# Value and output-gate projections as seven half-block products in an early stage of a hybrid encoder block

## The chip, the cores and the metric

The kernel runs on one core of a Trainium2 chip. The metric is the device time of one launch in microseconds (us); the runs shown are given by their median. TensorE (PE in the profile) multiplies matrices into PSUM, an on-chip memory of eight banks of 128 x 512 fp32. VectorE (DVE) and ScalarE (ACT) do the elementwise work, GpSimd (POOL) and SyncE (SP) issue most of the transfers between DRAM and the on-chip SBUF.

## The reference: one hybrid encoder block

One layer over 512 positions of width 1024 in fp32. Three branches share one normalised input `h`; all their inputs come out of one wide projection. What this change touches are `sb_v`, `ml_v`, `ml_o` (1024 columns each), `ml_i`, `ml_f` (4 columns each) and the second third of `gate_pre`.

```python
h = _rmsnorm(x, g_mix[l])
z = h @ w_in[l]
(sb_q, sb_k, sb_v, ml_q, ml_k, ml_v, ml_o, ml_i, ml_f, x_q, gate_pre) = jnp.split(z, IN_SPLITS, axis=-1)
y_sb = stick_breaking(8 heads of 128: sb_q, sb_k, sb_v)
qk = jax.nn.silu(_causal_conv(jnp.concatenate([ml_q, ml_k], axis=-1), conv_w[l], conv_b[l]))
...
hm = _mlstm(4 heads of 256: mq, mk, ml_v, i_pre, f_pre)
hm = _rmsnorm(hm, ml_norm_g)
y_ml = hm * jax.nn.sigmoid(ml_o)
y_x = cross_attention(4 heads of 256: x_q, 256 memory tokens)
gates = jax.nn.sigmoid(gate_pre + b_gate[l]).reshape(bsz, seq, N_BRANCH, D_MODEL)
mixed = gates[:, :, 0] * (y_sb @ w_sb_proj) + gates[:, :, 1] * (y_ml @ w_ml_proj) + gates[:, :, 2] * (y_x @ w_x_proj)
x = x + mixed @ w_out[l]
u = _rmsnorm(x, g_mlp[l]) @ w_ff1[l]
x = x + jnp.square(jax.nn.relu(u)) @ w_ff2[l]
```

## The kernel before: one long queue of matmuls

Every fp32 operand is kept as a pair of a high and a low half (`whi`, `wlo` for weights, two planes of `h` for the input). ACT makes the high half by a copy, DVE the low half by a subtraction (`load_w`, L81 and L82; `split`, L93 and L94, with a scale L96 and L97). A product is then three matmuls, high by high, high by low and low by high (`mm3`, L86 to L88). A projection in the form `projT` gives 128 features x 512 positions in 24 matmuls of 512 columns. In the form `projN` it gives 512 positions x 256 features in 96 matmuls of 256 columns, with `h` as the stationary operand; the twelve calls of `projN` are the values of two stick-breaking heads each (`sb_v`, four), the mLSTM values (`ml_v`, four) and the mLSTM output gate (`ml_o`, four).

The stages follow each other on PE: keys and values of the memory tokens (to 56 us); cross-attention with its query projections `xq` and the third branch's gates (to 154); their output projection with the first branch's gates (to 220); stick-breaking, eight heads (to 417); the first branch's output projection (to 484); mLSTM, four heads (to 718); the second branch's output projection with four of its gates (to 785); then the last projection and the MLP, which already use seven half-block products in place of eight, by the function `product` (L735 to L737).

An mLSTM head consists of four query and key feature tiles f0 to f3 (`ml_qk`: projection into a bank `pj`, copied by ACT into `xs` at L608; a four-tap convolution into `u`, one step on ACT (L609) and three on DVE (L612); a sigmoid; the split `mqk`), the scores `st` with their decay `w`, `sc`, the numerators `nm`, a norm, and the product with the sigmoid of the output gate. The code of a head starts the next head's feature tiles before its own numerators, and the output-gate and value projections of the next head behind them. In head 3, gates of the second branch stand in both places. The input and forget gates are computed as eight further columns of the first `sb_v` projection, gathered in `gcol` and transposed ahead of mLSTM.

The program is written in the order of the stages; a scheduler with buffers of fixed number (`tag`, `bufs`) sets the order on each engine, and each engine then works strictly in that order. PSUM has two banks `pj`, four `q4` and two `tr`.

Of the kernel before, what the change touches and what calls it, by code (L numbers as in the profile page):

```python
# [15 lines left out]
P = 128  # L16
# [10 lines left out]
NI = HD + 8  # L27
WI = 4 * NI

# [7 lines left out]
def tile_block(ctx: ExitStack, tc: tile.TileContext, xT, x_, memT, mem_, small,  # L37
               w_sbqk, w_sbv0, w_sbv, w_mlqk, w_mlv, w_mlo, w_xq, w_gate, w_kv,
# [33 lines left out]
    def load_w(src, parts=1, raw=None):  # L72
        n = src.shape[-1]
        if raw is None:
            raw = wp.tile([P, WI], F32, tag="raw", bufs=3, name="raw")
        hi = wp.tile([P, WI], F32R, tag="whi", bufs=4, name="whi")
        lo = wp.tile([P, WI], F32R, tag="wlo", bufs=4, name="wlo")
        for i in range(parts):
            c = slice(i * n // parts, (i + 1) * n // parts)
            nc.sync.dma_start(out=raw[:, c], in_=src[:, c])  # L80
            act.activation(out=hi[:, c], in_=raw[:, c], func=AF.Copy)  # L81
            dve.tensor_tensor(out=lo[:, c], in0=raw[:, c], in1=f32(hi[:, c]), op=ALU.subtract)  # L82
        return hi, lo
# [29 lines left out]
    def projN(wsrc, out_of, n=HD):  # L113

        ws = [load_w(wsrc[c]) for c in range(2)]
        for i in range(NT):
            out = out_of(i)
            for k in range(NK):
                hi, lo = ws[k // 4]
                c = slice((k % 4) * n, (k % 4 + 1) * n)  # L120
                mm3(out, h[k][:, 0, i * P:(i + 1) * P], h[k][:, 1, i * P:(i + 1) * P],
                    hi[:, c], lo[:, c], k == 0, k == NK - 1)

# [15 lines left out]
    def sigmoid(out, src, b=0.0, nb=0.0):  # L139
# [5 lines left out]
        act.activation(out=out, in_=out, func=AF.Exp, bias=b)  # L145

# [31 lines left out]
    gcol = cp.tile([P, NT, 64], F32, tag="gcol", name="gcol")  # L178
    pool.memset(gcol, 0.0)
# [9 lines left out]
    def mem_tiles(c):  # L189
        mT = hp.tile([P, 2, M], F32, tag="gate", bufs=4, name="mT")  # L190
# [66 lines left out]
    def mem_k(g):  # L257
# [9 lines left out]
        for m in range(NM):  # L267
            r = rk[:, 2 * m:2 * m + 2]
            dve.tensor_scalar(out=r, in0=r, scalar1=rm[:, m:m + 1], scalar2=None, op0=ALU.mult)
            t = hp.tile([P, T], F32, tag="gate", bufs=4, name="kn")  # L270
# [30 lines left out]

    mixed = [None] * NK

    def gate(b, f):
        o = pj()
        projT(h, load_w(w_gate[b * NK + f]), o)
        g = hp.tile([P, T], F32, tag="gate", bufs=4, name="gate")
# [127 lines left out]
    def sb_v(g):  # L435
        vs[g] = [tp.tile([P, 2, HD], F32R, tag="v", bufs=6, name="v") for _ in range(NT - 1)]
        vs[g].append(tp.tile([P, HD], F32, tag="v3", bufs=2, name="v3"))
        if g == 0:

            po = [q4() for _ in range(NT)]  # L440
            projN(w_sbv0, lambda i: po[i][:, :NI], NI)
            for i in range(NT):
                sb_vi(g, i, po[i][:, :HD])
                dve.tensor_copy(out=gcol[:, i].rearrange("p (a b) -> p a b", a=2)[:, :, :4],
                                in_=po[i][:, HD:NI].rearrange("p (a b) -> p a b", a=2))
            return
        po = [pj(), pj()]
        projN(w_sbv[g - 1], lambda i: po[i // 2][:, (i % 2) * HD:(i % 2 + 1) * HD])
        for i in range(NT):
            sb_vi(g, i, po[i // 2][:, (i % 2) * HD:(i % 2 + 1) * HD])  # L450
# [67 lines left out]
    sb_v(0)  # L518
    sb_qk(0)
    sb_weights(0)  # L520
    gs, aT = [], None
# [19 lines left out]

    o = tr()
    for i in range(NT):
        pe.transpose(o[:64, i * P:(i + 1) * P], gcol[:, i], ident)
    ip, fp, fa, mf, fc = (tmp(n)[:4, :] for n in ("ip", "fp", "fa", "mf", "fc"))
    act.activation(out=ip, in_=o[0:4, :], func=AF.Identity, bias=sm[0:4, C_BIF:C_BIF + 1])
    act.activation(out=fp, in_=o[32:36, :], func=AF.Identity, bias=sm[32:36, C_BIF:C_BIF + 1])
# [33 lines left out]
    def ml_v(head):  # L581
        vs[head] = []
        po = [pj(), pj()]
        projN(w_mlv[head], lambda i: po[i // 2][:, (i % 2) * HD:(i % 2 + 1) * HD])
        for i in range(NT):
            t = tp.tile([P, 2, HD + 2], F32R, tag="v", bufs=8, name="v")
            split(t[:, 0, :HD], t[:, 1, :HD], po[i // 2][:, (i % 2) * HD:(i % 2 + 1) * HD])
# [3 lines left out]
    def ml_o(head):  # L591
        po = [tr(), tr()]
        projN(w_mlo[head], lambda i: po[i // 2][:, (i % 2) * HD:(i % 2 + 1) * HD])
        sos[head] = []
        for b in range(2):
            t = tp.tile([P, T], F32, tag="so", bufs=4, name="so")
            sigmoid(t, po[b])
            sos[head].append(t)

    def ml_qk(head):  # L600
        qk = qks.setdefault(head, [])
        for f in range(4):
# [3 lines left out]
            u, xs = tmp("u"), tmp("xs")  # L606
            cw = C_CW + 4 * ft
            act.activation(out=xs, in_=o, func=AF.Copy)  # L608
            act.activation(out=u, in_=xs, func=AF.Identity, scale=sm[:, cw + 3:cw + 4],  # L609
                           bias=sm[:, C_CB + ft:C_CB + ft + 1])  # L610
            for d in (1, 2, 3):
                dve.scalar_tensor_tensor(out=u[:, d:], in0=xs[:, :T - d], scalar=sm[:, cw + 3 - d:cw + 4 - d],  # L612
# [24 lines left out]
    for head in range(4):  # L637
# [32 lines left out]
        else:  # L670
            gs += [gate(1, 0), gate(1, 1)]
# [19 lines left out]
        yts = [tmp("yt") if head == 3 else hp.tile([P, T], F32, tag="gate", bufs=4, name="yt") for _ in range(2)]  # L691
        for i in range(NT):
            c = slice((i % 2) * HD, (i % 2 + 1) * HD)
            dve.scalar_tensor_tensor(out=yts[i // 2][:, c], in0=nms[i][:, :HD], scalar=dn[:, i:i + 1],
                                     in1=so[i // 2][:, c], op0=ALU.mult, op1=ALU.mult)
        if head < 3:
            ml_o(head + 1)
            ml_v(head + 1)
        else:
            gs += [gate(1, 2), gate(1, 3)]  # L700
# [10 lines left out]
    def w_pair(raw):  # L711
        hi = wp.tile([P, WI], F32R, tag="whi", bufs=4, name="whi")
        lo = wp.tile([P, WI], F32R, tag="wlo", bufs=4, name="wlo")
        act.activation(out=hi[:, :W], in_=raw, func=AF.Copy)  # L714
        dve.tensor_tensor(out=lo[:, :W], in0=raw, in1=f32(hi[:, :W]), op=ALU.subtract)  # L715
        return hi, lo

    def s_new():

        return [hp.tile([P, 4, 2 * P], F32R, tag="h", bufs=NK, name=n) for n in ("shi", "slo")]  # L720

    def s_pair(src):
        sp = s_new()
        split(*sp, src)
        return sp

    def product(banks, sp, ws, start, stop, after=lambda v: None, end=False):

        def one(j, k, c):
            st, sp_ = start and k == 0, stop and k == 3  # L730
            lh, ll = sp[0][:, k, j * P:(j + 1) * P], sp[1][:, k, j * P:(j + 1) * P]
            w = ws[k // 2]
            cw = slice((k % 2) * T + c.start, (k % 2) * T + c.stop)
            mm = dict(skip_group_check=True)
            pe.matmul(banks[j][:, c], lh, w[0][:, cw], start=st, stop=False, **mm)  # L735
            pe.matmul(banks[j][:, c], lh, w[1][:, cw], start=False, stop=False, **mm)  # L736
            pe.matmul(banks[j][:, c], ll, w[0][:, cw], start=False, stop=sp_, **mm)  # L737

        if end:

            for j, c in ((0, slice(0, T)), (1, slice(0, T // 2)), (1, slice(T // 2, T))):
                for k in range(4):
                    one(j, k, c)
            return
        for v in range(2):
            for j in range(2):
                for k in (2 * v, 2 * v + 1):
# [342 lines left out]
```

## Time and profile before

| | us |
|---|---|
| median of three runs | 1165.07 (1164.43 to 1166.15) |
| the profiled execution, its own time | 1165.21 |
| its span in the trace | 1162.8 |
| PE busy | 1153.2 (99%) |
| DVE busy | 709.7 (61%) |
| ACT busy | 641.1 (55%) |
| twelve head-wise projections, stretches on PE | 137.2 |
| mLSTM stage, 484 to 718 | 234.0 |

The granted TensorE clock is 0.999 of full speed in this execution. The trace gives each instruction's start and duration. On PE neighbouring matmuls overlap, so a group's summed duration is more than the time it takes; the length of a stretch of the timeline is the better measure. For DVE and ACT, too, the distance between two starts in a row is shorter than the duration shown (by about 0.1 us). Times are counted from the start of the span.

### The profile page before, as it was taken

How to read it: one execution, taken by the hardware profiler on the slowest of the kernel's cores; microseconds unless marked ns; L12 is line 12 of the kernel's file. 1: busy time of each engine (PE TensorE's matmuls, PEld its weight loads, DVE VectorE, ACT ScalarE, POOL GpSimd, SP SyncE). 2: the span in 40 equal slices, each digit the busy share in tenths (PEclk: the TensorE clock that was granted, in tenths of full speed). 3: DMA queues.
4: the chain of work that ended last, by engine and by line, in shares of the span. 5: the costliest groups of instructions: out<-in, count | busy, mean ns of one | idle time of the engine just before them, and what ended most of it. 6: DMA issues, size and time to landing. Idle time of an engine off the chain costs nothing.

```text
span 1162.8 us, 15156 instructions
## 1 busy us (share of the span) xinstructions
PE 1153.2 (99%) x5844; PEld 970.9 (83%) x5844; DVE 709.7 (61%) x1112; ACT 641.1 (55%) x1085; POOL 58.5 (5%) x100
## 2 busy tenths in 40 slices
PE   9999999999999999999999999999999999999998
PEld 6788888888988888898989898888888888888887
DVE  5966633357567753475677765479638448458457
ACT  7955544246556754276767666445645354454443
POOL 0000000000000000010000000001001001011010
PEclk9999999999999999999999999999999999999999
DMA  9631223232222222323222225648547548448244
GB/s 361 225 115 45 73 81 102 73 109 74 73 74 73 73 91 93 93 78 109 82 91 79 86 73 178 206 109 207 165 96 177 170 106 200 145 102 208 89 72 109
DMA packets 40687, 138.45 MB, mean 119 GB/s; under 512 B 4516, under 2 KB 4900, under 8 KB 40616
## 3 DMA queue, kind: packets, MB, share of 16 engines
q1 hardware_dynamic: 34712, 116.45, 30.0%
q0 software_dynamic: 5760, 20.97, 10.2%
q8 instruction: 46, 0.75, 0.3%
q14 instruction: 25, 0.20, 0.1%
q10 hardware_dynamic: 144, 0.07, 0.0%
HBM read 135.37 MB, written 2.11 MB: 118 GB/s over the span
## 4 chain that ended last, share of the span: by engine, by line
PE 94%; DMA 2%; DVE 2%; ACT 1%; issue 1%; SPq 0%; DVEq 0%; ACTq 0%
PE pj L88 16%; PE pj L87 16%; PE pj L86 16%; PE q L86 7%; PE q L87 6%; PE q L88 6%; PE q L737 3%; PE q L736 3%; PE q L735 3%; PE tr L86 2%; PE tr L88 2%; PE tr L87 2%; PE pj L737 2%; PE pj L736 2%; PE pj L735 2%; DMA xrow<-in_x_dram 1%
## 5 line engine op out<-in xcount | busy, mean ns | idle before, releaser
L82 DVE TENSOR_TENSOR wlo<-raw,whi 128x1024 fp32r<-128x1024 f32 x148 | 180.6, 1223 | 209.3 <-ACT whi L81 197.7
L81 ACT ACTIVATE whi<-raw 128x1024 fp32r<-128x1024 f32 x148 | 156.3, 1060 | 240.4 <-PE pj L87 159.5
L86 PE MATMUL pj<-h,whi 128*128 128x512 f32 x512 | 202.4, 395 | 0.0
L87 PE MATMUL pj<-h,whi 128*128 128x512 f32 x512 | 201.3, 393 | 0.0
L88 PE MATMUL pj<-h,wlo 128*128 128x512 f32 x512 | 201.2, 393 | 0.0
L714 ACT ACTIVATE whi<-rq 128x1024 fp32r<-128x1024 f32 x70 | 74.3, 1061 | 110.5 <-PE q L87 43.6
L715 DVE TENSOR_TENSOR wlo<-rq,whi 128x1024 fp32r<-128x1024 f32 x70 | 85.5, 1221 | 76.1 <-ACT whi L714 75.9
L88 PEld LDWEIGHTS pj<-h,wlo 128*128 128x128 f32 x512 | 96.3, 188 | 21.0 <-issue 0.5
L86 PEld LDWEIGHTS pj<-h,whi 128*128 128x128 f32 x512 | 96.5, 189 | 20.0
L87 PEld LDWEIGHTS pj<-h,whi 128*128 128x128 f32 x512 | 96.3, 188 | 19.9
L88 PE MATMUL q<-x1g,wlo 128*128 128x512 f32 x240 | 94.2, 393 | 0.0
L86 PE MATMUL q<-x1g,whi 128*128 128x512 f32 x240 | 94.2, 392 | 0.0
L87 PE MATMUL q<-x1g,whi 128*128 128x512 f32 x240 | 94.1, 392 | 0.0
L86 PE MATMUL pj<-y,whi 128*128 128x512 f32 x192 | 75.8, 395 | 0.0
L88 PE MATMUL pj<-y,wlo 128*128 128x512 f32 x192 | 75.6, 394 | 0.0
L87 PE MATMUL pj<-y,whi 128*128 128x512 f32 x192 | 75.5, 393 | 0.0
L737 PE MATMUL q<-whi,slo 128*128 128x512 f32 (+1 forms) x164 | 63.5, 387 | 0.0
L735 PE MATMUL q<-whi,shi 128*128 128x512 f32 (+1 forms) x164 | 63.5, 387 | 0.0
L736 PE MATMUL q<-wlo,shi 128*128 128x512 f32 (+1 forms) x164 | 63.4, 387 | 0.0
L86 PE MATMUL pj<-whi,h 128*128 128x256 f32 x224 | 63.3, 283 | 0.0
L88 PE MATMUL pj<-whi,h 128*128 128x256 f32 x224 | 63.1, 282 | 0.0
L87 PE MATMUL pj<-wlo,h 128*128 128x256 f32 x224 | 63.0, 281 | 0.0
(344 smaller groups left out, 2372.2 us busy)
## 6 DMA issues: line engine op xcount, KB each, us to landing
raw<-in_w_ff_dram SPq DMA_DIRECT2D x32, 512.0 KB, 3.7
rq<-in_w_ff_dram SPq DMA_DIRECT2D x32, 512.0 KB, 5.1
rq<-in_w_ff_dram POOLq DMA_DIRECT2D x32, 512.0 KB, 5.4
raw<-in_w_gate_dram SPq DMA_DIRECT2D x24, 512.0 KB, 3.5
raw<-in_w_proj_dram SPq DMA_DIRECT2D x24, 512.0 KB, 3.6
raw<-in_w_sbqk_dram SPq DMA_DIRECT2D x16, 512.0 KB, 3.5
raw<-in_w_mlqk_dram SPq DMA_DIRECT2D x16, 512.0 KB, 3.5
rawk<-in_w_kv_dram SPq DMA_DIRECT2D x10, 512.0 KB, 9.0
```

Of the source, the lines that this page charges most:

```text
L81: act.activation(out=hi[:, c], in_=raw[:, c], func=AF.Copy)
L82: dve.tensor_tensor(out=lo[:, c], in0=raw[:, c], in1=f32(hi[:, c]), op=ALU.subtract)
L86: pe.matmul(out, lh, rh, start=start, stop=False)
L87: pe.matmul(out, lh, rl, start=False, stop=False)
L88: pe.matmul(out, ll, rh, start=False, stop=stop)
L714: act.activation(out=hi[:, :W], in_=raw, func=AF.Copy)
L715: dve.tensor_tensor(out=lo[:, :W], in0=raw, in1=f32(hi[:, :W]), op=ALU.subtract)
L735: pe.matmul(banks[j][:, c], lh, w[0][:, cw], start=st, stop=False, **mm)
L736: pe.matmul(banks[j][:, c], lh, w[1][:, cw], start=False, stop=False, **mm)
L737: pe.matmul(banks[j][:, c], ll, w[0][:, cw], start=False, stop=sp_, **mm)
```

## The change: an early stage, three matrices at once

Behind the memory keys and ahead of the query projections stands a new stage that computes three matrices of 512 x 1024, `sb_v`, `ml_v` and `ml_o`, each as a product of `h` with a 1024 x 1024 weight. Both are cut into two halves each way, and the four blocks of the result come out of seven products of half size (24 matmuls of 512 columns each) by sums of blocks before and after. Sums of weights are made in part by accumulating transfers (`w_more`, on POOL's queue) and in part on DVE (`sums`); sums of `h` halves by DVE (`s_form`, once for all three matrices), for which the scaled `h` is kept in fp32 in `xts`. The results are combined by ACT and DVE (`V`, `X`, `v_out`) and written to DRAM on POOL's queue; the third matrix goes through the sigmoid on the way. The stages that need a head's columns read them back (`vr`, `so`, 128 x 4 x 256, on SP's queue).

The input and forget gates become one product of their own, ahead of mLSTM: a stationary operand of 100 columns that holds the high and the low halves of both gates' weights (`wif`), 16 matmuls of 512 columns. The convolution reads the projection's bank directly, without `xs`. The gates of the second branch, `gate(1, 0)` to `gate(1, 7)`, stand between the mLSTM heads: 0 and 1 behind the numerators of head 0, 2 behind head 1, 3 behind head 2, 4 to 7 in head 3. In the second branch's output projection, where four of them stood, none are left. `gate` tiles get eight buffers in place of four.

```diff
@@ h_tile @@
-        hf = tmp("hf")
-        dve.tensor_tensor(out=hf, in0=xts[k], in1=rx, op=ALU.mult)
+        dve.scalar_tensor_tensor(out=xts[k], in0=xts[k], scalar=sm[:, C_GMIX + k:C_GMIX + k + 1], in1=rx,
+                                 op0=ALU.mult, op1=ALU.mult)
         t = hp.tile([P, 2, T], F32R, tag="h", bufs=NK, name="h")
-        split2(t, hf, sm[:, C_GMIX + k:C_GMIX + k + 1])
+        split2(t, xts[k])
...
@@ the new stage @@
+    def s_form(S, op, in0, in1, tag="h"):
+        sp = s_new(tag)
+        for k in range(4):
+            dve.tensor_tensor(out=S[:, k], in0=in0(k), in1=in1(k), op=op)
+            s_tile(sp, k, S[:, k])
+        return sp
+    def w_more(raws, w, fh, kh):
+        for v in range(2):
+            pool.dma_start(out=raws[v], in_=w[fh, 2 * kh + v], accum_op=ALU.add)
+    def v_out(b, th, fh, j, make):
+        t = tmp("vo")
+        make(t)
+        if b == 2:
+            g = tmp("so")
+            sigmoid(g, t)
+            t = g
+        i = 2 * th + j
+        pool.dma_start(out=rows[b][i * P:(i + 1) * P, fh * T:(fh + 1) * T], in_=t)
+    def v_first(b):
+        B3 = v_raw(b, 1, 1, lambda: ring("B3"))
+        w_more(B3, w_vo[b], 1, 0)
+        B11 = v_raw(b, 0, 0, lambda: ring("B11"))
+        return B3, B11
+    nxt = v_first(0)
+    sp3 = s_form(S, ALU.subtract, hf(0, 0), hf(0, 1), "y")
+    sp5 = s_form(S, ALU.subtract, hf(1, 1), hf(0, 1), "y")
+    for b in range(3):
+        B3, B11 = nxt
+        if b == 0:
+            w11 = w_pairs(B11)
+            w3 = w_pairs(B3)
+        a, c, d, e = [pj(), pj()], [q4(), q4()], [q4(), q4()], [tr(), tr()]
+        product(a, hA(0, 0), w11, True, False)
+        w_more(B11, w_vo[b], 1, 0)
+        B22 = v_raw(b, 1, 1, lambda: wp.tile([P, W], F32, tag="raw", bufs=3, name="B22"))
...
+        for j in range(2):
+            act.activation(out=V[j], in_=a[j], func=AF.Copy)
+        product(c, sp3, w3, True, False)
+        w5 = w_pairs(B11)
+        B21 = v_raw(b, 0, 1, lambda: tp.tile([P, W], F32, tag="B21", bufs=2, name="B21"))
...
+        product(d, sp5, w5, True, False)
+        sums(B11, B22)
+        if b == 0:
+            sp6 = s_form(S, ALU.add, lambda k: S[:, k], hf(0, 0), "y")
+        w6 = w_pairs(B11)
...
+        product(e, sp6, w6, True, True)
+        w21 = w_pairs(B21)
+        product(a, hA(1, 0), w21, False, True)
+        sums(B11, B21)
+        w4 = w_pairs(B11)
...
+        product(c, hA(1, 1), w4, False, True)
+        if b == 0:
+            sp4 = s_form(S, ALU.subtract, lambda k: S[:, k], hf(1, 0), "y")
+        w22 = w_pairs(B22)
+        if b < 2:
+            nxt = v_first(b + 1)
+        for j in range(2):
+            v_out(b, 0, 0, j, lambda t: act.activation(out=t, in_=a[j], func=AF.Copy))
+        product(d, sp4, w22, False, True)
...
@@ stick-breaking, values @@
-        po = [pj(), pj()]
-        projN(w_sbv[g - 1], lambda i: po[i // 2][:, (i % 2) * HD:(i % 2 + 1) * HD])
+        raw = tp.tile([P, NT, HD], F32, tag="vr", name="vr")
+        nc.sync.dma_start(out=raw, in_=rows[0][:, g * HD:(g + 1) * HD].rearrange("(i p) c -> p i c", p=P))
@@ ahead of mLSTM @@
-    for i in range(NT):
-        pe.transpose(o[:64, i * P:(i + 1) * P], gcol[:, i], ident)
+    for k in range(NK):
+        pe.matmul(o[:NG, :], wif[:, k], h[k][:, 0, :], start=k == 0, stop=False)
+        pe.matmul(o[:NG, :], wif[:, k], h[k][:, 1, :], start=False, stop=k == NK - 1)
@@ mLSTM @@
-        po = [tr(), tr()]
-        projN(w_mlo[head], lambda i: po[i // 2][:, (i % 2) * HD:(i % 2 + 1) * HD])
...
+        nc.sync.dma_start(out=t, in_=rows[2][:, head * HD:(head + 1) * HD].rearrange("(i p) c -> p i c", p=P))
...
-            act.activation(out=xs, in_=o, func=AF.Copy)
-            act.activation(out=u, in_=xs, func=AF.Identity, scale=sm[:, cw + 3:cw + 4],
+            act.activation(out=u, in_=o, func=AF.Identity, scale=sm[:, cw + 3:cw + 4],
...
-                dve.scalar_tensor_tensor(out=u[:, d:], in0=xs[:, :T - d], scalar=sm[:, cw + 3 - d:cw + 4 - d],
+                dve.scalar_tensor_tensor(out=u[:, d:], in0=o[:, :T - d], scalar=sm[:, cw + 3 - d:cw + 4 - d],
...
         if head < 3:
+            gs += [gate(1, f) for f in ((0, 1), (2,), (3,))[head]]
             ml_o(head + 1)
             ml_v(head + 1)
```

What this makes of the engines' order shows at three places. The first is DVE at the start of the new stage. `vm` and `kk` are the last tiles of the memory tokens, `S` and `slo` the sums of `h` halves and their low halves, `B_652` and `B_653` the first product's weights, `B_646` and `B_647` the second's:

```order
L153 TENSOR_TENSOR S<-xt 128x256 x3
L139 TENSOR_TENSOR wlo<-B_652,whi 128x1024
L93 TENSOR_TENSOR slo<-S,shi 128x256
L96 SCALAR_TENSOR_TENSOR vm<-tr,rm,vm 128x512 x2
...
L96 SCALAR_TENSOR_TENSOR kk<-q_637,sm,kk 128x256
L93 TENSOR_TENSOR slo<-S,shi 128x256
L139 TENSOR_TENSOR wlo<-B_653,whi 128x1024
L153 TENSOR_TENSOR S<-xt 128x256 x3
L93 TENSOR_TENSOR slo<-S,shi 128x256 x3
L153 TENSOR_TENSOR S<-xt 128x256
L139 TENSOR_TENSOR wlo<-B_646,whi 128x1024
```

In the kernel before, two weight tiles of the query projections stood ahead of `vm` and a third among the `kk`; here the sums and the weights of two products stand around them.

The second is ACT where cross-attention begins, in the kernel of the change. `so` are the steps of the third matrix's sigmoids, `qT` and `sqq` read the banks of the first and second query projection:

```order
L129 ACTIVATE so<-vo 128x512
L95 ACTIVATE qT<-pj,sm 128x512
L133 ACTIVATE so<-so 128x512
L130 ACTIVATE so<-so 128x512
L129 ACTIVATE so<-vo 128x512
L131 ACTIVATE so<-so 128x512
L130 ACTIVATE so<-so 128x512
L496 ACTIVATE sqq<-pj 128x512
L133 ACTIVATE so<-so 128x512
L131 ACTIVATE so<-so 128x512
L95 ACTIVATE qT<-pj,sm 128x512
```

Before, `sqq` followed `qT` with at most a weight tile between. Now sigmoid steps stand ahead of `qT` and between it and `sqq`.

The third is PE at the scores of the first mLSTM head. Before, they stood behind the last value or output-gate projection:

```order
L87 MATMUL tr<-wlo,h 128x256
L88 MATMUL tr<-whi,h 128x256
L86 MATMUL q_4815<-mqk 128x512
L87 MATMUL q_4815<-mqk 128x512
L88 MATMUL q_4815<-mqk 128x512
```

In the kernel of the change they stand inside the second feature tile of the next head, whose first tile has just been issued behind this head's f3:

```order
L85 MATMUL pj<-h,whi 128x512
L86 MATMUL pj<-h,whi 128x512
L85 MATMUL q_5135<-mqk 128x512
L86 MATMUL q_5135<-mqk 128x512
L85 MATMUL q_5142<-mqk 128x384
L86 MATMUL q_5142<-mqk 128x384
L85 MATMUL q_5149<-mqk 128x256
L86 MATMUL q_5149<-mqk 128x256
L799 MATMUL q_5156<-qk_4969,qk_5065 128x128
L87 MATMUL q_5135<-mqk 128x512
```

Where two projections of 96 matmuls separated f3 from the scores, one feature tile and the start of another do now; in heads 1 to 3 the numerators and one or two gates do.

More of the change, by code (lines that the diff above doesn't have):

```diff
@@ L74, in load_w @@
         if raw is None:
[L75 to L77 removed]
+            raw = wp.tile([P, W], F32, tag="raw", bufs=3, name="raw")
+        hi = wp.tile([P, W], F32R, tag="whi", bufs=4, name="whi")
+        lo = wp.tile([P, W], F32R, tag="wlo", bufs=4, name="wlo")
         for i in range(parts):
@@ L300, in tile_block, with hA, tiles, hf @@
         mem_kT(kn)
+    rows = [dp.tile([T, D], F32, tag=n, name=n) for n in ("sbv", "mlv", "mlo")]
+    def hA(kh, th):
+        def tiles(k, j):
+            c = slice((2 * th + j) * P, (2 * th + j + 1) * P)
+            return h[4 * kh + k][:, 0, c], h[4 * kh + k][:, 1, c]
+        return tiles
+    def hf(kh, th):
+        return lambda k: xts[4 * kh + k][:, 2 * th * P:2 * (th + 1) * P]
+    def v_raw(b, fh, kh, where):
+        raws = [where() for _ in range(2)]
+        for v in range(2):
+            nc.sync.dma_start(out=raws[v], in_=w_vo[b, fh, 2 * kh + v])
+        return raws
@@ new lines, in ring, with sums @@
+    def ring(name):
+        return tp.tile([P, W], F32, tag="qT", bufs=4, name=name)
+    def sums(raws, more):
+        for v in range(2):
+            dve.tensor_tensor(out=raws[v], in0=raws[v], in1=more[v], op=ALU.add)
+    def v_out(b, th, fh, j, make):
[7 more added lines that the diff above has]
+        pool.dma_start(out=rows[b][i * P:(i + 1) * P, fh * T:(fh + 1) * T], in_=t)
@@ L591, in ml_o @@
     def ml_o(head):
-        po = [tr(), tr()]
-        projN(w_mlo[head], lambda i: po[i // 2][:, (i % 2) * HD:(i % 2 + 1) * HD])
[L594 to L598, printed above, removed]
+        t = tp.tile([P, NT, HD], F32, tag="so", bufs=2, name="so")
+        nc.sync.dma_start(out=t, in_=rows[2][:, head * HD:(head + 1) * HD].rearrange("(i p) c -> p i c", p=P))
+        sos[head] = t
     def ml_qk(head):
@@ L690, in tile_block @@
         dve.tensor_tensor(out=dn, in0=rr, in1=dn, op=ALU.mult)
-        yts = [tmp("yt") if head == 3 else hp.tile([P, T], F32, tag="gate", bufs=4, name="yt") for _ in range(2)]
+        yts = [tmp("yt") for _ in range(2)]
         for i in range(NT):
@@ L709, in tile_block @@
     u = [None] * NK
[L711 to L747, printed above, removed]
-                    one(j, k, slice(0, T))
-            after(v)
     def w_raw(w, fh, kh):
@@ L756, in w_raw @@
         return raws
-    def w_more(raws, w, fh, kh):
-        for v in range(2):
-            pool.dma_start(out=raws[v], in_=w[fh, 2 * kh + v], accum_op=ALU.add)
-    def w_pairs(raws):
-        return [w_pair(raw) for raw in raws]
     def stile(name):
@@ L839, in out_proj @@
         product(c, sp3, w3, True, False)
-        V = [hp.tile([P, T], F32, tag="gate", bufs=4, name="V") for j in range(2)]
+        V = [hp.tile([P, T], F32, tag="gate", bufs=NK, name="V") for j in range(2)]
         for j in range(2):
@@ L900, in norm1 @@
         dve.tensor_scalar(out=nr2, in0=r2, scalar1=-1.0, scalar2=None, op0=ALU.mult)
-    V = [hp.tile([P, T], F32, tag="gate", bufs=4, name="V") for j in range(2)]
+    V = [hp.tile([P, T], F32, tag="gate", bufs=NK, name="V") for j in range(2)]
     def onto(th, fh, src, minus, j, cs=slice(0, T)):
```

147 lines of the change are left out of this document (92 added, 55 removed).

## The prediction

> **What bounds the kernel now.** I read the page's engine shares, then the waits of TensorE, then the busy time by stage.
>
> ```profile
> span 1162.8 us, 15156 instructions
> PE 1153.2 (99%) x5844; PEld 970.9 (83%) x5844; DVE 709.7 (61%) x1112; ACT 641.1 (55%) x1085; POOL 58.5 (5%) x100
> ...
> PE tr L496 <- DVE aT L94: 1.3, 3, 0.4
> PE q L86 <- ACT hm L96: 1.2, 1, 1.2
> ...
> 0.00:60.00 60.00, 55.79 (x236) 41.83 (x237) 45.98 (x89) 49.37 (x94) 2.02 (x12) 1.00 0.78 290
> ...
> 220.00:417.00 197.00, 195.70 (x1122) 170.11 (x1121) 123.78 (x224) 116.18 (x242) 8.44 (x16) 1.00 0.24 75
> ...
> 484.00:718.00 234.00, 234.00 (x1489) 212.68 (x1488) 157.08 (x304) 157.12 (x300) 12.78 (x31) 1.00 0.28 89
> 718.00:785.00 67.00, 67.00 (x297) 54.89 (x295) 38.61 (x60) 31.51 (x49) 4.55 (x5) 1.00 0.59 173
> 785.00:1162.00 377.00, 373.83 (x1653) 305.79 (x1651) 232.17 (x258) 183.61 (x235) 30.48 (x35) 1.00 0.56 142
> ```
>
> The two rows in the middle are waits (total, times, longest). The last five give a stretch and its length, then the busy time of PE, PEld, DVE, ACT and POOL, the granted clock, the share of the DMA engines and GB/s; a stretch of PE alone has the same ends. From 60 us on TensorE (PE) hardly stops; the mLSTM stage (484 to 718) has not one idle us in 234.00. So taking work from PE pays in full, unless a wait appears that this work covered. No other engine is full over a whole stage, so the question is local: which chains were hidden behind the removed projections? The profiled execution took 1165.21 us, the median of the runs is 1165.07; the sum is made against the first, and 0.14 us between them changes nothing.
>
> **The PE work.** Matmuls overlap in the pipeline, so a duration is not a price; the length of a stretch is. Twelve stretches hold the twelve head-wise projections (96 matmuls of 256 columns each); six stretches of the output projection each hold one half-block product of 24 matmuls of 512 columns, the form that the change uses.
>
> ```profile
> 219.88:231.49 11.61, 11.61 (x97) 1.00 0.14 45
> ...
> 676.13:687.54 11.41, 11.41 (x98) 1.00 0.29 93
> sum 137.17, PE 137.17; mean PE 11.43
> ...
> 790.42:795.94 5.52, 5.52 (x25) 1.00 0.98 277
> ...
> 806.99:812.52 5.53, 5.53 (x25) 1.00 0.80 187
> 812.52:818.04 5.52, 5.52 (x25) 1.00 1.04 288
> sum 33.15, PE 33.15; mean PE 5.53
> ```
>
> Removed: 137.2 us. Added: 21 products of 5.53 = 116.1 us, and for the input and forget gates 16 matmuls of 512 columns at 5.53/24 = 0.23, 3.7 us; four transposes of 128 columns (about 0.1 each, half of 0.23) leave, 0.4. Net: 137.2 − 116.1 − 3.7 + 0.4 = **17.8 us less**. The three waits on aT, 1.3 us together, each stand behind a head that held a value projection, and should go: 19.1. The moved gates cost PE the same wherever they stand.
>
> **The start of the new stage.** Its first three products want two sets of activation sums (each four subtractions and four low halves of 256 columns) and six weight tiles split. Here stand three such stretches, then rows of the timeline, which give start and length.
>
> ```profile
> 28.66:55.10 26.44, 24.66 (x103) 18.39 (x102) 24.97 (x45) 23.84 (x49) 0.00 (x0) 1.00 0.62 226
> 55.10:67.46 12.36, 12.36 (x62) 10.26 (x60) 8.82 (x13) 7.32 (x13) 0.00 (x0) 1.00 0.70 213
> 386.75:402.80 16.05, 16.05 (x84) 13.37 (x82) 12.81 (x25) 13.62 (x29) 0.47 (x1) 1.00 0.20 66
> ...
> 55.93 1.40 DVE L97 SCALAR_TENSOR_TENSOR vm<-tr,rm,vm 128x512 fp32r<-128x512 f32 x2
> 57.25 1.65 DVE L97 SCALAR_TENSOR_TENSOR kk<-q,sm,kk 128x256 fp32r<-128x256 f32 x4
> ...
> 557.04 1.21 DVE L82 TENSOR_TENSOR wlo<-raw,whi 128x1024 fp32r<-128x1024 f32 x1
> 558.17 0.68 DVE L94 TENSOR_TENSOR mqk<-u,mqk 128x512 fp32r<-128x512 f32 x1
> ```
>
> Just before this point (28.66 to 55.10) VectorE (DVE) is busy 24.97 of 26.44 us, and still owes some 3 to 4.5 us of memory work (the vm and kk rows start after 55.9). A weight split paces at 558.17 − 557.04 = 1.13; the 256-column operations at 1.65/4, 0.4 or a little less. The new demand is 16 × 0.37 + 6 × 1.13 = 12.7; with 4 owed, 16.7 us of DVE stand against two products of cover, 11.1, and about 1.5 for the last split and subtractions that product three needs only in its second half. A shortfall near 4. PE's order puts the matmuls that need only high halves ahead of the others, at most two thirds of a product, so part of it is covered: I take **2.5** (0.5 if nearly all is, 4.5 if nothing). Within a branch 38.7 us of PE stand against 14 splits and 4 weight sums at 1.13 and ten result steps near 0.6, 26.3 of DVE, so the steady state should hold.
>
> Transfers: a branch loads twelve half-megabyte tiles and writes 2.1 MB, 8.4 MB in 38.7 us, 217 GB/s. The output projection's stretches above carried 277 and 288 in a like mix without a stall: taken as nothing.
>
> **The entry of cross-attention.** The third branch's eight result tiles pass through the sigmoid, four ScalarE (ACT) operations each, queued ahead of the first query's qT.
>
> ```profile
> 555.51 1.04 ACT L81 ACTIVATE whi<-raw 128x1024 fp32r<-128x1024 f32 x1
> 556.46 0.61 ACT L93 ACTIVATE mqk<-u 128x512 fp32r<-128x512 f32 x1
> 557.08 0.64 ACT L141 ACTIVATE sg<-u 128x512 f32<-128x512 f32 x1
> 557.62 0.58 ACT L608 ACTIVATE xs<-pj 128x512 f32<-128x512 f32 x1
> 558.10 0.62 ACT L142 ACTIVATE sg<-sg 128x512 f32<-128x512 f32 x1
> 558.62 0.80 ACT L609 ACTIVATE u<-xs,sm 128x512 f32<-128x512 f32 x1
> ```
>
> The pace is 0.52 (558.10 to 558.62) and 0.95 for a weight. Between the first result (two products, 11.1 us, before the stage's end) and qT the new order has two copies, some 26 sigmoid steps and five weights: 28 × 0.52 + 5 × 0.95 = 19.3, so qT starts 8.2 us after the stage's end where its projection is done at 5.5. The bank is free only after the square, six operations on, near 12; the third projection wants it at 11.1. With the second query and the softmax behind it **3.0** (0.5 to 5).
>
> **Stick-breaking.** Its values now come back from DRAM by loads on SP's queue. A head without value projection already runs with DVE 12.81 of 16.05 and PE full (the 386.75 row); the splits, about 1.7 us, fit. Nothing; 2 if that cover is gone.
>
> **mLSTM.** Per head 22.8 us of output-gate and value projections leave, which stood between the query and key features (f0 to f3) and the scores; one or two gates take their place. And the convolution now reads the projection's bank itself, so that one of two banks is held to the third DVE step instead of a copy.
>
> ```profile
> 555.04 0.28 PE L86 MATMUL q<-v,sc 128*128 128x258 f32 x1
> ...
> 559.46 0.75 DVE L612 SCALAR_TENSOR_TENSOR u<-xs,sm,u 128x511 f32<-128x511 f32 x1
> 560.12 0.69 DVE L144 SCALAR_TENSOR_TENSOR sg<-u,sg 128x512 f32<-128x512 f32 x1
> 560.73 0.74 DVE L612 SCALAR_TENSOR_TENSOR u<-xs,sm,u 128x510 f32<-128x510 f32 x1
> ...
> 562.17 0.74 DVE L612 SCALAR_TENSOR_TENSOR u<-xs,sm,u 128x509 f32<-128x509 f32 x1
> ...
> 568.69 0.55 DVE L94 TENSOR_TENSOR mqk<-u,mqk 128x384 fp32r<-128x384 f32 x1
> ...
> L144 DVE SCALAR_TENSOR_TENSOR sg<-u,sg 128x512 f32<-128x512 f32 x16 | 11.0, 688 | 16.0 <-ACT sg L143 15.9
> ...
> L144 DVE SCALAR_TENSOR_TENSOR so<-tr,so 128x512 f32<-128x512 f32 x8 | 5.5, 685 | 8.7 <-ACT so L143 8.7
> ```
>
> Feature f3's projection ends at 555.04. Its low half is done at 569.24, 14.2 later; without the copy 13.7. In the new order the second half of the first scores comes 11.0 after f3: **2.3** lost there. For the next heads the cover is 11.8, 12.6 and 12.6, and the low half is wanted 0.7 after the first score: 1.2, 0.4, 0.4, **2.0**. The bank: the copy ended at 558.20 (3.2 after the projection), the third convolution step at 562.91 (7.9, or 7.4 without the copy), and PE wants it back after one more projection, 5.5. Numerators or scores stand between in most places; about 0.4 per head for f1's bank and more in head 0, where eight projections follow each other: **2.5**. mLSTM: 6.8, taken as **7**. DVE and ACT lose work here (weights, output-gate sigmoids), which may shorten the chains to almost no wait; the copy gone from each of 16 tiles may lengthen the holds: bounds 1 and 14.
>
> On the price of reading the bank: the same operation, line and size takes 685 ns from PSUM (so<-tr) and 688 from SBUF (sg<-u), so I add nothing. [...]
>
> The later stages keep PE's work and order, with proj(1) (718 to 785) now bare of gates: DVE was at 38.61 of 67.00 with them.
>
> **Sum:** −17.8 − 1.3 + 2.5 + 3.0 + 7 = −6.6, so 1165.2 − 6.6 = **1158.6 us**.
>
> **Rivals.**
> *All hidden.* The scheduler's interleaving and the lighter DVE and ACT cover the waits: 1.5 us of them, 1165.2 − 19.1 + 1.5 = 1147.6. For it: mLSTM's DVE is at 157.08 of 234.00. Against: the start has DVE full and cover counted above.
> *The banks set the beat of mLSTM (slower).* If each of f1 to f3 in four heads waits the whole 7.4 − 5.5 = 1.9, that is 12 × 1.9 = 22.8 in place of 7: 1165.2 − 19.1 + 5.5 + 22.8 = 1174.4. It decides slower from 13.6 us of waits in mLSTM (19.1 − 5.5), 0.85 per feature tile. Against: DVE needs 1.13 for a weight, 3 × 0.67 for the convolution and 3 × 0.6 for the rest, 4.9 us of each 5.5 us tile, so its queue should not grow. [...]
> *The early stage is paced by transfers.* If its mix of accumulating loads and writes gets the 187 GB/s of the 806.99 stretch, 8.4 MB takes 45 us, 6.2 more per branch, 18.6 in three: 1177.2. Against: that stretch did not stall, and had no more to carry. From 205 GB/s upward (41 us) it would cost under 7 and leave the result at no change or better.
>
> **Chances.** The forecast's case 0.57 (its own range 1152 to 1165), all hidden 0.22, banks 0.14, transfers 0.07. A difference under 0.2% (2.3 us) can't be told from none. In the forecast's case 0.82 is faster, 0.16 the same; the two slower rivals keep 0.04 of same between them. Faster 0.57 × 0.82 + 0.22 = 0.69; same 0.09 + 0.04 = 0.13, taken 0.14; slower 0.17. The range reaches from the hidden case to the forecast's upper bounds and a little of the banks: 1147 to 1169, leaving out some 0.2.
>
> **What would show it.** PE's busy time near 1135 and some 21 us of idle in the span (1162.8 − 1153.2 = 9.6 now); waits of the first products on low halves (L93, L139) of 2 to 3 us; of the third query projection's first matmul on ACT; of scores on mqk and of projections on L762 in mLSTM, near 7 together. A product far from 5.5 us, or waits on DMA in the early stage, would prove me wrong; so would mLSTM without waits (then 1148), or with more than 14.

## The result, and the profile after

The changed kernel takes 1145.28 us, median of four runs (1143.70 to 1146.04), beside 1164.99 for the kernel before (1164.43 to 1166.15): a ratio of 0.983, with a 95% interval of 0.981 to 0.985. That is 19.7 us less. The forecast was 1158.6, and 1147 to 1169 for the range, so the time lies below both. The profiled execution took 1143.7 us (span 1141.9 and 1.8 around it).

First the page of the changed kernel, its first lines, then its waits of TensorE (total, times, longest):

```profile
span 1141.9 us, 14192 instructions
PE 1126.8 (99%) x5208; PEld 930.4 (81%) x5208; DVE 772.7 (68%) x1203; ACT 664.0 (58%) x1122; POOL 79.9 (7%) x135
...
PE pj L86 <- DVE wlo L81: 2.5, 1, 2.5
PE q L171 <- DVE wlo L139: 1.5, 1, 1.5
PE q L85 <- DVE yt L844: 1.4, 3, 0.6
PE warm L232 <- DVE wz L202: 1.2, 1, 1.2
PE pj L171 <- DVE wlo L139: 0.9, 1, 0.9
PE pj L85 <- DVE u L762: 0.7, 1, 0.7
PE pj L85 <- DVE gt L476: 0.7, 1, 0.7
PE tr L642 <- DVE aT L93: 0.6, 2, 0.3
```

New waits are there. Two rows were forecast (L139 at the start of the new stage, L762 in mLSTM). Two were not: the longest of all (L81, 2.5 us at 30 us, in the memory stage) and L844, where scores wait for a bank of the numerators, which is free only after the step `yt`. For scores that wait on `mqk`, which the forecast did name, there is no row. PE's idle time has grown from 9.6 to 15.1 us. But PE's busy time fell by 26.4 us (1153.2 to 1126.8), where the sum of matmuls taken away and added gave 17.8. The length of each stage, from its first matmul to the first of the next, tells where:

| stage (us) | before | after | difference |
|---|---|---|---|
| memory tokens | 55.9 | 57.6 | +1.7 |
| new stage | | 118.5 | +118.5 |
| cross-attention | 97.7 | 97.1 | −0.6 |
| third branch's projection | 66.3 | 65.3 | −1.0 |
| stick-breaking, with the input and forget gates' product | 197.4 | 153.4 | −44.0 |
| first branch's projection | 66.4 | 66.4 | 0.0 |
| mLSTM | 234.8 | 167.8 | −67.0 |
| second branch's projection | 66.4 | 43.6 | −22.8 |
| output projection and MLP, to the last matmul's end | 373.9 | 368.5 | −5.4 |

The last row has the same instructions in both kernels, and is 5.4 us shorter. The third branch's projection has the same ones too, and is 1.0 shorter. No wait of the kernel before explains this, since it had none there. The matmuls themselves have become faster. The view of stretches of PE shows it best where four feature tiles of 24 matmuls of 512 columns follow each other, at the end of the third branch's projection. Before:

```profile
197.80:203.39 5.59, 5.59 (x26) 1.00 0.29 94
203.39:208.84 5.45, 5.45 (x25) 1.00 0.27 96
208.84:214.43 5.59, 5.59 (x25) 1.00 0.31 94
214.43:219.88 5.45, 5.45 (x25) 1.00 0.29 99
sum 22.08, PE 22.08; mean PE 5.52
```

And after:

```profile
316.78:322.22 5.44, 5.44 (x25) 1.00 0.26 96
322.22:327.66 5.44, 5.44 (x25) 1.00 0.29 96
327.66:333.10 5.44, 5.44 (x25) 1.00 0.29 99
333.10:338.54 5.44, 5.44 (x25) 1.00 0.28 96
sum 21.76, PE 21.76; mean PE 5.44
```

Before, tiles of 5.59 and 5.45 alternate; after, all take 5.44. The granted clock is 1.00 in all eight. Over the whole trace, the distance from the start of a 512-column matmul to the next start, where no wait stands between, is 230.2 ns before (3959 pairs) and 227.2 after (4446).

What alternates is the buffer of the weights. Before, `whi` and `wlo` are rings of four buffers, 4224 bytes apart in each partition (1056 columns, which the first value projection with its eight gate columns needed). In the program's allocation they start at 192, 64, 192 and 64 modulo 256, and the activation tiles (`h`, `y`, `x1g`, `shi`) all at 64. Sorted by this, matmuls whose two operands start alike modulo 256 come at 227 to 230 ns apart, and those that differ by 128 at 232 to 233, whichever of the two is the stationary operand. The change narrowed the rings to 4096 bytes, because the wide tiles were no longer needed, and the weight and activation tiles now all start at 192. That is the theory that the first four experiments test.

### The profile page after: what moved, and what is told of

It is laid out like the page before. It is cut to its first block, busy times and chain, and to the rows that moved or that the text cites. A ratio compares the mean times of both kernels' runs of the same rounds, so it can differ in the third digit from the quotient of the medians.

```text
span 1141.9 us, 14192 instructions
## 1 busy us (share of the span) xinstructions
PE 1126.8 (99%) x5208; PEld 930.4 (81%) x5208; DVE 772.7 (68%) x1203; ACT 664.0 (58%) x1122; POOL 79.9 (7%) x135
## 4 chain that ended last, share of the span: by engine, by line
PE 55%; DVE 3%; ACT 2%; issue 1%; DMA 0%; DVEq 0%; ACTq 0%; POOLq 0%
PE pj L85 7%; PE pj L86 7%; PE pj L87 7%; PE q L85 6%; PE q L86 5%; PE q L87 5%; PE q L171 3%; PE q L170 3%; PE q L172 3%; PE pj L170 2%; PE pj L171 2%; PE pj L172 2%; DVE u L762 1%; DVE wlo L81 1%; PE tr L170 1%; PE tr L171 1%
## 5 line engine op out<-in xcount | busy, mean ns | idle before, releaser
L81 DVE TENSOR_TENSOR wlo<-raw,whi 128x1024 fp32r<-128x1024 f32 x124 | 151.2, 1222 | 151.0 <-ACT whi L80 142.5
L80 ACT ACTIVATE whi<-raw 128x1024 fp32r<-128x1024 f32 x124 | 130.7, 1058 | 175.5 <-PE pj L86 116.7
L139 DVE TENSOR_TENSOR wlo<-rq,whi 128x1024 fp32r<-128x1024 f32 x70 | 85.4, 1220 | 74.7 <-ACT whi L138 74.5
L171 PE MATMUL q<-wlo,shi 128*128 128x512 f32 (+1 forms) x236 | 91.1, 386 | 1.5 <-DVE wlo L139 1.5
L172 PE MATMUL q<-whi,slo 128*128 128x512 f32 (+1 forms) x236 | 91.0, 386 | 0.0
L170 PE MATMUL q<-whi,shi 128*128 128x512 f32 (+1 forms) x236 | 90.7, 386 | 0.0
L138 ACT ACTIVATE whi<-B 128x1024 fp32r<-128x1024 f32 x42 | 44.4, 1061 | 44.1 <-PE q L172 16.9
L139 DVE TENSOR_TENSOR wlo<-B,whi 128x1024 fp32r<-128x1024 f32 x42 | 50.9, 1221 | 19.3 <-ACT whi L138 19.3
L171 PEld LDWEIGHTS q<-wlo,shi 128*128 128x128 f32 x236 | 44.3, 188 | 10.8 <-DVE wlo L139 2.0
```

The lines of the kernel that those rows point to most:

```text
L138: act.activation(out=hi, in_=raw, func=AF.Copy)
L139: dve.tensor_tensor(out=lo, in0=raw, in1=f32(hi), op=ALU.subtract)
```

## The experiments

### The place of the operands

Two theories stand against each other. **Place**: the pace of a matmul depends on where its two operands start relative to each other. **Work alone**: the whole gain is the removed matmuls with nearly all new waits hidden, and the pace belongs to something else of the kernel before.

The changed kernel with the old spacing of the weight halves:

```diff
+WI = 1056
...
-        hi = wp.tile([P, W], F32R, tag="whi", bufs=4, name="whi")
-        lo = wp.tile([P, W], F32R, tag="wlo", bufs=4, name="wlo")
+        hi = wp.tile([P, WI], F32R, tag="whi", bufs=4, name="whi")[:, :W]
+        lo = wp.tile([P, WI], F32R, tag="wlo", bufs=4, name="wlo")[:, :W]
...
```

> The changed kernel with its weight-half tiles (whi, wlo) spaced 4224 bytes apart again, as in the kernel before, and nothing else: every second buffer then starts 128 bytes off a multiple of 256 from the activation tiles. Theory (place of the operands): matmuls of 512 columns whose weight tile and activation tile differ by 128 bytes modulo 256 pace at about 232.7 ns, the others at 227, so the mean goes from 227 to about 230 and the time from 1145.3 by 4600 x 3.0 ns = 13.6 us to about 1159. Rival (the gain is the removed work alone, the new waits being hidden): 1145, pace 227.

Measured: 1160.56 us (0.9959 of the kernel before, 0.9945 to 0.9974). The same four tiles alternate again:

```profile
319.74:325.20 5.46, 5.46 (x26) 1.00 0.28 96
325.20:330.79 5.59, 5.59 (x26) 1.00 0.28 94
330.79:336.24 5.45, 5.45 (x25) 1.00 0.30 96
336.24:341.83 5.59, 5.59 (x25) 1.00 0.29 97
```

So at the old spacing, all that the change does to the work and its order is worth 1165.33 − 1160.56 = 4.8 us; the other 15.3 us come from the spacing. The old spacing isn't quite the old pace, though: the mean distance here is 231.4 ns, where the kernel before has 230.2. The product of the input and forget gates takes one buffer of the `whi` ring and none of `wlo`, so that from 502 us on the two halves of each weight start 128 bytes apart from each other. Matmuls that start alike then stand among others that don't, and come at 230.2 ns over the trace, in place of 227.8 before. So 4.8 us is a low figure for the work; the next run gives another.

The kernel before, with only its ring spacing changed to a multiple of 256 bytes (that of the tiles `raw` too, which hold the weights before the split):

```diff
-WI = 4 * NI
+WI = 1088
```

> The kernel before with its weight tiles spaced 4352 bytes (17 x 256) apart in place of 4224, and nothing else; all weight and activation tiles then have the same address modulo 256. Theory (place of the operands): all 512-column matmuls at 227 ns, 4100 x 3.2 ns = 13 us less, about 1152. Rival (pace belongs to something else of the kernel before): 1165.

Measured: 1154.98 (0.9913, 0.9898 to 0.9928), 10.3 us less than before without one instruction changed. The same four tiles:

```profile
197.73:203.17 5.44, 5.44 (x26) 1.00 0.30 96
203.17:208.61 5.44, 5.44 (x26) 1.00 0.31 96
208.61:214.05 5.44, 5.44 (x26) 1.00 0.34 99
214.05:219.49 5.44, 5.44 (x26) 1.00 0.32 96
```

It falls 3 us short of the expectation. The twelve projections of 256-column matmuls became 1.1 us longer in all (119.1 ns from start to start before, 119.9 here), and the memory stage is 1.1 us longer too. With all tiles alike in both kernels, the work and its order are worth 1154.98 − 1145.28 = 9.7 us. In this run the starts of the operands differ by 0 or by 256 modulo 512, and all pace alike (5.44 us for each of the four tiles), so the period is 256 bytes here, not 512.

Then 128 and 64 bytes put between the weight tiles and everything behind them:

```diff
+    pad = hp.tile([P, 32], F32, tag="pad", bufs=1, name="pad")
+    pool.memset(pad, 0.0)
     wz = hp.tile([P, T], BF16, tag="tmp", bufs=6, name="wz")
```

> The changed kernel with 128 bytes put between the weight tiles and all activation tiles: every pair then differs by 128 modulo 256. Theory (relative place): all pairs at 232.7 ns, 4600 x 5.7 ns = 26 us more, about 1171. Rival (it is an absolute start, of the weight tile alone, that counts): weight tiles have not moved, so 1145.

> The same with 64 bytes in place of 128. If only a difference of 128 modulo 256 costs, 1145; if any difference costs, about 1171; if cost grows with the difference, about 1158.

Measured: 1165.81 with 128 bytes and 1157.44 with 64. With 128, the weights have not moved, and every tile is slow:

```profile
322.59:328.16 5.57, 5.57 (x26) 1.00 0.29 94
328.16:333.74 5.58, 5.58 (x25) 1.00 0.26 94
333.74:339.31 5.57, 5.57 (x25) 1.00 0.30 97
339.31:344.89 5.58, 5.58 (x25) 1.00 0.28 94
```

It is the relative start that counts. The mean distance is 232.6 ns, 5.4 more than in the changed kernel; over some 4600 matmuls 25 us, of which 20.5 show in the time. Of the rest, 1.7 us is idle time of PE that the slower matmuls cover (13.4 for 15.1 in the profiles). With that pad the changed kernel is no faster than the kernel before (1.0005, 0.9995 to 1.0015). With 64 bytes the mean is 230.8, but unevenly: 233.3 where the weights are the moving operand, 227.7 to 231.6 where they are the stationary one. Between 0 and 128 the cost therefore isn't a simple slope. Why two operands that start differently slow each other is not shown by any run here.

### The terms of the sum: copies, sigmoids, gates

Differences here and below are to the changed kernel's first median, 1145.28, unless another is named.

The copy of the convolution's input, restored in the changed kernel:

```diff
-            u = tmp("u")
+            u, xs = tmp("u"), tmp("xs")
+            act.activation(out=xs, in_=o, func=AF.Copy)
...
-            act.activation(out=u, in_=o, func=AF.Identity, scale=sm[:, cw + 3:cw + 4],
+            act.activation(out=u, in_=xs, func=AF.Identity, scale=sm[:, cw + 3:cw + 4],
...
-                dve.scalar_tensor_tensor(out=u[:, d:], in0=o[:, :T - d], scalar=sm[:, cw + 3 - d:cw + 4 - d],
+                dve.scalar_tensor_tensor(out=u[:, d:], in0=xs[:, :T - d], scalar=sm[:, cw + 3 - d:cw + 4 - d],
```

> The changed kernel with the convolution's copy xs on ScalarE restored (16 copies in mLSTM), all else as changed. The prediction's term: banks are held to the third DVE step, 2.5 us of waits, which the copy would remove; it puts 0.5 us into each tile's chain, about 0.5 us more at each of four scores, 2.0 us: together 0.5 us less, about 1145. Rival (the held banks set the beat of mLSTM): 6 us less or more, 1139. Other rival (ScalarE's chain is the limit): 4 us more or above, 1149.

Measured: 1151.65 (0.9888, 0.9868 to 0.9907). Not the half microsecond less of the prediction's terms, but 6.4 more: to read the bank without the copy is a gain here. mLSTM is 7.1 us longer (174.9 for 167.8), most of it in one place. This run's waits of PE have a row that the changed kernel's have not:

```profile
PE pj L85 <- DVE gate L132: 4.2, 1, 4.2
```

A gate's bank was held 4.2 us too long: between the second step of its sigmoid on ACT (620.5 us) and the third (625.3) stood four sigmoid steps of a feature tile, a split and the squares of the numerators. After the wait, the granted clock was 0.50 from 627 to 633 us, which at half pace loses 3.4 us more. Wait and slow clock make up the 7.1 us of the stage. So the third theory (ACT's chain is the limit) came nearest, although its 4 us were too few; how sixteen copies lead to this one late sigmoid was not taken apart.

The output gate's matrix first, so that its sigmoids run inside the early stage:

```diff
-    rows = [dp.tile([T, D], F32, tag=n, name=n) for n in ("sbv", "mlv", "mlo")]
+    rows = [dp.tile([T, D], F32, tag=n, name=n) for n in ("mlo", "sbv", "mlv")]
...
-        if b == 2:
+        if b == 0:
...
```

> The changed kernel with the three matrices in another order: the output gate's first, so that its sigmoids run inside the early stage and not at its end; nothing else. Theory (the sigmoids at the end delay the first query projection's exit, 1.5 to 3 us): 2 us less, about 1143. Rival (ScalarE had room at the end and is short inside the stage): no change or slower, 1145 to 1148.

Measured: 1151.10 (0.9880, 0.9866 to 0.9895), 5.8 more. Cross-attention became 0.6 us shorter (96.6 for 97.1), and no more than that do the sigmoids cost there where the change has them. The early stage became 7.5 us longer (126.0 for 118.5): inside it they hold up a weight at 114 us, and the waits show it:

```profile
PE q L170 <- ACT whi L138: 4.8, 1, 4.8
```

After this wait the granted clock was 0.50 for 3.4 us, from 119 us on.

The second branch's gates where the kernel before had them:

```diff
-            gs += [gate(1, 4), gate(1, 5)]
+            gs += [gate(1, 0), gate(1, 1)]
...
-            gs += [gate(1, f) for f in ((0, 1), (2,), (3,))[head]]
...
-            gs += [gate(1, 6), gate(1, 7)]
+            gs += [gate(1, 2), gate(1, 3)]
```

> The changed kernel with the second branch's gates where the kernel before had them (0 to 3 in head 3, 4 to 7 in the second branch's output projection), all else as changed. Theory (the gates are cover for the chain from feature tile to score, 13.7 us): in heads 1 to 3 only the numerators, 3.6 us, are left as cover, so about 9.4 us are lost per head in place of 0.7, 26 us more, about 1171. Rival (the scheduler fills the gap with other work, or the chain shortens because PE leaves DVE and ACT free): 1150 or less.

Measured: 1155.03 (0.9918, 0.9894 to 0.9942), 9.7 more than the changed kernel. The gates are cover, as the theory has it, but for less than the 26 us; the time lies between theory and rival. The waits in mLSTM that grew:

```profile
PE q L85 <- DVE yt L844: 4.3, 2, 3.5
...
PE pj L85 <- DVE u L762: 2.0, 3, 1.1
...
PE q L85 <- ACT sc L92: 1.4, 1, 1.4
PE q L85 <- ACT mqk L92: 1.3, 1, 1.3
```

The theory's chain ends in `mqk`, and that row has 1.3 us in all, where 9.4 per head were expected. The longest wait, 3.5 us ahead of the second head's scores, is for a bank of the numerators, free after `yt`, and was followed by 3.4 us at a granted clock of 0.50; neither theory names it. That the chain itself became shorter, as the rival says, was not measured.

### The order of VectorE's work at the start

The longest new wait stands at 30 us, in the memory stage, where the prediction had none: DVE scales two input tiles (`xt`, L335, 1.4 us) before it makes the low half that PE waits for. The stretches of PE around it, in the changed kernel:

```profile
29.85:33.05 3.20, 0.73 (x2) 1.00 1.04 397
33.05:34.33 1.28, 1.27 (x4) 0.80 1.06 410
34.33:37.10 2.77, 2.77 (x8) 0.50 1.03 407
37.10:40.00 2.90, 2.90 (x13) 0.98 1.02 407
```

After 2.5 us of idling, eight matmuls ran at a granted clock of 0.50, at 427 ns for 227: 1.6 us more. Four runs turn the order on DVE; a fifth is the changed kernel itself, for comparison. The scaling behind the low halves:

```diff
+    los = []
...
-            dve.tensor_tensor(out=lo[:, c], in0=raw[:, c], in1=f32(hi[:, c]), op=ALU.subtract)
+            los.append(dve.tensor_tensor(out=lo[:, c], in0=raw[:, c], in1=f32(hi[:, c]), op=ALU.subtract))
...
-        dve.scalar_tensor_tensor(out=xts[k], in0=xts[k], scalar=sm[:, C_GMIX + k:C_GMIX + k + 1], in1=rx,
-                                 op0=ALU.mult, op1=ALU.mult)
+        with tc.issue_after(lov[k // 2].ins):
+            dve.scalar_tensor_tensor(out=xts[k], in0=xts[k], scalar=sm[:, C_GMIX + k:C_GMIX + k + 1], in1=rx,
+                                     op0=ALU.mult, op1=ALU.mult)
...
+    lov = los[-4:]
```

> The changed kernel with the in-place scaling of the input tiles queued on DVE behind the low weight halves of the memory values, which PE wants first; nothing else. In the trace of the change PE waits 2.5 us there (at 30 us) and then runs eight matmuls at 427 ns in place of 227. Theory (DVE order, and the slow matmuls follow from the idle time): 2 us of the wait and 1.6 us of slow matmuls go, 3.5 us less, about 1142. Rival (the same DVE work is only late elsewhere, at the new stage's start): 1145.

Measured: 1150.18 (0.9875, 0.9858 to 0.9892), 5 us more. The wait at 30 us shrank to 0.7, but the scheduler then put the sums of input halves ahead of the new stage's first weights:

```profile
PE pj L173 <- DVE wlo L141: 4.6, 1, 4.6
```

and the granted clock was 0.50 from 66 to 73 us, and from 56 to 59 behind two waits of 0.8. The rival was nearer: the work was late elsewhere, and at a worse place. So the second edit, the weights of the first two products ahead of the sums, with the first edit and without:

```diff
     nxt = v_first(0)
+    w11 = w_pairs(nxt[1])
     S = tp.tile([P, 4, 2 * P], F32, tag="S", name="S")
     sp3 = s_form(S, ALU.subtract, hf(0, 0), hf(0, 1), "y")
+    w3 = w_pairs(nxt[0])
...
-        if b == 0:
-            w11 = w_pairs(B11)
-            w3 = w_pairs(B3)
```

> The run with the late scaling, with one more edit: the first two products' weights are split ahead of the sums of input halves (in the program's order), since in that run DVE made the sums and the memory tiles first and the weight's low half came 4.9 us late. Theory (at the start DVE's order alone decides, and an idle gap of more than 2 us is paid once more by matmuls at half pace): both waits go, 3 to 4 us less than the changed kernel, about 1142. Rival (DVE's amount of work up to 67 us decides, in whatever order): 1145 or above.

> The second edit alone: the changed kernel with the first two products' weights split ahead of the sums, the scaling as changed. Theory (order): the waits of 1.1 and 1.7 us at 62 and 66 us shrink, the one of 2.6 us at 30 us and its slow matmuls stay, 1 to 2 us less than the changed kernel, about 1144. Rival (amount of work): 1145.

And both edits with the last memory values' splits moved behind the second product's weights:

```diff
...
     w3 = w_pairs(nxt[0])
+    mem_vs(1, vo1)
...
```

> Both edits, and the splits of the last memory values (vm, 1.4 us of DVE) behind the second product's weights, since cross-attention needs them only 100 us later. Theory (order): 1 us less than with both edits, about 1141. Rival (amount of work): no change against both edits.

> The changed kernel itself once more, beside the three runs on DVE's order: 1145.3 by its first runs; all theories alike.

Measured, all on one chip:

| kernel | median us | ratio to before, interval |
|---|---|---|
| the changed kernel again | 1146.53 (1143.80 to 1149.82) | 0.9838 (0.9818 to 0.9858) |
| weights first | 1142.53 (1141.82 to 1147.64) | 0.9811 (0.9792 to 0.9829) |
| weights first, late scaling | 1143.71 (1142.91 to 1148.83) | 0.9822 (0.9803 to 0.9840) |
| both edits, and late memory values | 1144.49 (1143.72 to 1149.50) | 0.9828 (0.9810 to 0.9846) |

The medians favour the weights first, by 4.0 us over the changed kernel beside it and by 2.8 over its first median. But single executions of these kernels differ by 4 to 6 us, and the intervals overlap: that it beats the changed kernel is likely, not shown. In its profile, which is of the slowest of its five executions (1147.64), the waits at the new stage's start fell from 1.5 and 0.9 us to 1.0 us in three pieces, but the entry of cross-attention has one of 1.4 (`sqq`) in place of 0.3. Neither the late scaling nor the late memory values added to the gain. Here DVE's order moves waits about more than it removes them. The 2 us that one expectation gives for a gap that costs matmuls at half pace was the author's estimate: in the second profile of the changed kernel a gap of 2.5 us at 31 us was followed by a granted clock of 1.00.

That speaks for the rival, the amount of work up to 67 us, but does not show it, for DVE isn't full there. In the changed kernel it idles 1.0 us just ahead of the low half that PE waits 1.5 us for at 66.6:

```profile
64.09 1.06 ACT L138 ACTIVATE whi<-B 128x1024 fp32r<-128x1024 f32 x1 [2.64 <-DMA B<-in_w_vo_dram]
65.05 1.01 ACT L92 ACTIVATE shi<-S 128x256 fp32r<-128x256 f32 x3
...
65.48 1.10 DVE L93 TENSOR_TENSOR slo<-S,shi 128x256 fp32r<-128x256 f32 x3 [1.01 <-ACT shi L92]
66.50 0.42 DVE L153 TENSOR_TENSOR S<-xt 128x256 f32<-128x256 f32 x1
66.83 1.22 DVE L139 TENSOR_TENSOR wlo<-B,whi 128x1024 fp32r<-128x1024 f32 x1
```

ACT waits 2.6 us for a weight of the third product, the sum that an accumulating transfer (issued at 57.34 on POOL) makes, and the high halves `shi` stand behind it on ACT, the low halves `slo` behind those on DVE, and the second product's weight last. So a transfer has its part in this wait; no run moves that weight or that transfer.

## Why the prediction was right or wrong

**The bound** was read rightly: PE sets the time, before and after (99% busy in both), and what counts is work taken from it minus waits that appear.

**The step that failed** is the price of PE's work: "21 products of 5.53 = 116.1 us", and "The later stages keep PE's work and order", which put the change there at nothing. The prediction took PE's price per matmul from the kernel before and held it for fixed through the change. The edit of the weight tiles from 1056 to 1024 columns, which the prediction did not mention, changed that price for every 512-column matmul in the program: a product takes 5.44, and what was not touched is faster too (the last stages by 5.4 us). By the runs this is worth 15.3 us in the changed kernel (1160.56 − 1145.28) and 10.3 in the kernel before (1165.33 − 1154.98). Less these 10.3, the forecast would have been 1148.3, 3.0 above the result. The signs that the prediction names show the same: PE's busy time is 1126.8, not near 1135, and PE idles 15.1 us, not 21. The rows to see it by were there: the four tiles of the third branch's projection at 5.59 and 5.45 in turn, as the starts of the ring's buffers alternate modulo 256. The prediction took an average where the trace showed two values.

**The rest of the sum** came out near, at either pace: 6.6 us less was forecast, 4.8 was measured at the old spacing (1160.56 against 1165.33) and 9.7 with all tiles alike (1145.28 against 1154.98). The waits one by one can be read from the second pair, which has one pace: each is the length of a stage in the changed kernel less that stage in the kernel before at even spacing, corrected for the work that left or came.

| term | forecast | measured | how |
|---|---|---|---|
| memory stage | 0 | +0.6 | 57.6 − 57.0; +1.7 beside the kernel before as it was; late low half and halved clock, not foreseen |
| start of the new stage | +2.5 | +3.8 | 118.5 − 21 × 5.44 − 0.5 for four transposes that moved here |
| entry of cross-attention | +3.0 | +0.4 | 97.13 − (97.25 − 0.5 for these transposes) |
| waits on aT in stick-breaking | −1.3 | −0.6 | 153.4 − (197.1 − 46.3 − 0.4 + 3.6) |
| first branch's projection | 0 | +0.9 | 66.4 − 65.5; the row of L476, not foreseen |
| mLSTM | +7 | +4.0 | 167.8 − (234.1 − 8 × 11.51 + 4 × 5.44) |
| sum | +11.2 | +9.1 | |

Not all of this is idle time in PE's rows: mLSTM has 2.3 us of it and the new stage 2.9, and where the rest lies was not taken apart. The two profiled executions also differ by 2.9 us more than the medians (1156.34 and 1143.70), so the sum is no better than that. The sum agrees better than its terms do, which were off by one to three microseconds each way: that is luck. In mLSTM the mechanism was not the forecast one either: the scores' wait for f3's low half, 4.3 us of the 7, has no row, and the bank that is free after `yt` (1.4) was not named. The entry was too dear; the run with the output gate's matrix first finds 0.6 us for the sigmoids there. The aT waits did not all go with the value projections: a row of 0.6 us is left of 1.3.

**The rival "all hidden"** has a time, 1147.6, that is within 2.3 us of the result, and is still wrong: about 9 us of waits did appear. Time alone would have passed it for right; the run with the old spacing tells it apart, since "all hidden" has nothing to say about 15 us that come back with 32 columns of unused memory per tile. **The banks rival** did not come about: the row of L762 has 0.7 us. **Transfers** did not set the pace of the early stage, whose 118.5 us hold only 3.8 of waits; PE's rows there name DVE, although a transfer stands behind part of one of them. The chance of faster, 0.69, went to the side that came, and would have without the spacing too (4.8 to 9.7 us); that the gain is twice to four times as large came from an edit that the forecast left out.

**On reading PSUM** the prediction added nothing to the sum, by one pair of means. The trace of the change agrees: the convolution's three steps take 741 to 743 ns from PSUM (L762), beside 745 to 750 from the copy in SBUF before (L612), and the copy put back cost 6.4 us in all.

## What to carry to other kernels

When a change alters the size of a buffer, look at where all later buffers start: on a program bound by TensorE, operands that start alike modulo 256 bytes were worth 10 to 15 us of 1165 here, more than the removed work less the waits that it brought (5 to 10). Two values in turn in a row of equal stretches are a finding, not noise to be averaged. And a time close to a rival's is no proof of the rival: hold one part of the change fixed and measure it.

## What the runs showed of the hardware that was not expected

- 512-column matmuls in fp32r came 227.2 ns apart when the stationary and the moving operand start at the same byte modulo 256, and 232.6 when they differ by 128 (two kernels and one, 3900 to 4500 pairs each). In the changed kernel with the old spacing, where both kinds stand among each other, matmuls that start alike came 230.2 ns apart, in the kernel before 227.8. 256-column matmuls showed no such gain: in the kernel before they came 118.9 ns apart where the two start alike and 119.1 where they differ by 128 (539 pairs each).
- Between the first and the last matmul of these profiles, a granted clock of 0.50 lasted 3.41 or 6.83 us at a time, and came after idle time of PE. All eight gaps of 2.6 to 4.8 us were followed by it, two of the four of 2.5 us (in the first profile of the changed kernel, not in the second), and three of the many of 1.2 to 2.2 us, and once it came behind two gaps of 0.8. So a gap of 2.6 us or more was paid with 1.7 or 3.4 us on top, and a shorter one only sometimes; some of the difference between single executions may come from there.
